# Last two expert pairs combined on chip by fp32r products, and the accumulating fetch issued one pair earlier

## The chip, the cores and the metric

The kernel runs on one core of one Trainium2 chip. The metric is the device time of one execution in microseconds (us), lower is better. Times come from repeated executions, and the stages are read from one execution that the hardware profiler recorded, with every instruction and every DMA packet.

## What is computed

Two layers of a diffusion transformer with 256 context and 512 latent tokens of width 1024. Each layer is a token mixer (recurrences and gated branches) followed by a mixture of 32 experts in which every token goes to two experts. The last layer keeps the 512 latent tokens alone. The part that matters here:

```python
def hier_moe(t, ...):                       # t: 768 tokens in layer 0, 512 in layer 1
    ...                                     # router: two experts and two weights per token
    def block_fn(args):
        e, tok = args
        xb = t_pad[tok]
        return (jax.nn.silu(xb @ w_gate[e]) * (xb @ w_up[e])) @ w_down[e]
    yb = lax.map(block_fn, (blk_e, slot_tok.reshape(n_blocks, MOE_BLOCK)))
    y = jnp.zeros((N + 1, D), F32).at[slot_tok].add(yb.reshape(-1, D).astype(F32) * slot_w[:, None])
    return y[:N]
...
xl = xl + mod_l[:, 5] * y                   # and, after layer 1, rmsnorm(xl, final_norm_g)
```

## The kernel before

Tokens lie in SBUF as `x2`, six tiles of 128 tokens by 1024 (four in layer 1). Each expert has 64 slots, and two experts make a pair, so there are 16 pairs (`NP`) of 128 slots. `moe` loops over the pairs. For a pair `j` the engines do this:

- SyncE (SP) streams the weights: for each pair six units of 2 MB (`unit`, L265: two for the first half of gate and up, two for the second, two for the down product) into a ring of tiles called `u` and `m`. The two down units of the last pair are split into pieces of 512 KB.
- TensorE (PE) computes gate and up into `gu` (L666), then the rows of pair `j + 1` are gathered by products with a 0/1 matrix `oh` (`gather`, tags `ext` and `ew`), then transposes of the hidden rows (`eht`, L677), then the down product `ey` (L685). `pair` runs in this order; the two `next(mid, None)` in it are where the work of the generator `mid` is put between gate/up and down.
- VectorE (DVE) scales the result by routing weight and modulation (`scale`, L843), and a POOL queue DMA stores it as 128 rows of `ys` in DRAM (L849, L854).

After the last pair but one, the outputs of pairs 0 to 14 lie in `ys`. `combine_most` then issues the *fetch*: for each of a token's two choices and each tile of tokens one indirect DMA on POOL's queue (L884) that reads 128 rows of `ys` and adds them to a tile of `x2`. That is 12 DMAs in layer 0 and 8 in layer 1, of 512 KB each. A choice that is not in `ys` reads the zero row `NYS`. The outputs of the last pair stay on chip: `oh` is transposed to `ohT`, and PE multiplies it with the scaled rows in plain fp32 (L866), six (four) tiles times two halves of 512 columns, and DVE adds each result to `x2` (L1301). These additions come after the fetch into the same tile.

Behind the experts of layer 0 comes the norm of layer 1 (`norm_next`) and its first projection. Behind those of layer 1 comes `combine`: squares on ScalarE (ACT), a few small DVE steps, a scaling of each tile and the store of the output (L1014). POOL multiplies two of the four tiles by the norm's gain ahead of time (L1005), so that ACT can scale those two while DVE scales the others.

A scheduler may interleave work that is independent; `pin` keeps an instruction in its place in the written order.

Of the kernel before, what the change touches and what calls it, by code (L numbers as in the profile page):

```python
# [21 lines left out]
D = 1024  # L22
# [15 lines left out]
NYS = NMAIN - 2 * CAP  # L38
# [20 lines left out]
class B:  # L59
# [121 lines left out]
    def layer(self, l):  # L181
# [5 lines left out]
        with pool(f"pp{l}", space=PSUM) as self.pp:  # L187
# [13 lines left out]
            with pool(f"hin{l}") as self.hp:  # L201
# [11 lines left out]
                cols = lambda t: t.rearrange("p a (b c) -> p (a b) c", c=256)  # L213
                M = []
                for g in self.groups:
                    if self.whole(g):
                        t = cols(self.buf(*g))
                        M.append((t[:, :KD], t[:, KD:]))
                    else:
                        M.append([cols(self.half(g, x)) for x in "ab"])  # L220
# [32 lines left out]
    def half(self, g, x):  # L253
        return g[0].tile([128, 2, 1024], F32R, name=g[1] + x)
# [31 lines left out]
    def merge(self, l, n, y, M):  # L286
        nc, d = self.nc, self.d
        hs = [(0, 384), (384, 384)] if n == T else [(0, 512)]
        with self.pool(f"mg{l}") as yp:
            y.append(self.y_in(7, n, yp))  # L290
            for dt in range(KD):
# [19 lines left out]
                for g, m in enumerate(M):  # L311
                    self.split(m[0][:, dt], m[1][:, dt], acc[:, 256 * g:256 * g + 256])
# [8 lines left out]
    def post(self, l, M):  # L321
# [4 lines left out]
        with self.pool(f"po{l}") as p:  # L326
# [33 lines left out]
            for lo in range(i0, NT, n):  # L360
# [12 lines left out]
                for dt in range(KD):  # L373
# [28 lines left out]
                    self.mm3(ps, [(wh[:, k, :], wl[:, k, :], M[g][0][:, k], M[g][1][:, k]) for k in range(KD)])  # L402
# [38 lines left out]
    def route(self, lo, n, p, pp, rows, lt, rb, ss, hook):  # L441
# [30 lines left out]
        if (lo - i0) % 4 == 0:  # L472
            g = self.groups[(lo - i0) // 4]
            self.low.append(self.buf(*g) if self.whole(g) else self.half(g, "a"))
# [97 lines left out]
        nc.vector.scalar_tensor_tensor(a, e2, E_ - 2.5, a, ALU.is_gt, ALU.max)  # L572
# [186 lines left out]

    def gather(self, j, oh, xr, xT, pp):  # L760
# [8 lines left out]
        self.nxt = xT, sw  # L769
        yield  # L770
# [26 lines left out]
    def moe(self, l, ew, mst):  # L797
        tc, nc, d, wp = self.tc, self.nc, self.d, self.wp
        cs = self.conds
        with self.pool(f"moep{l}", space=PSUM) as pp, self.pool(f"ewC{l}") as ewC:  # L800
# [29 lines left out]
            xr = self.thirds(rows.rearrange("p a b -> p (a b)") if l else self.r(self.half(self.groups[1], "b"))[:, 0])  # L830
            for j in range(NP):
                xT, sw = self.nxt
                if j + 1 < NP:
                    self.onehot(j + 1, oh, range(nt))
                    self.beside(j + 1, range(nt))
                    mid = self.gather(j + 1, oh, xr, xn, pp)
                else:
                    mid = self.combine_most(self.r(oh), pp)
                    next(mid)
                py = self.pair(xT, self.units[6 * j:6 * j + 6], wp, pp, mid, lambda i: load(n + 6 * j + 2 * i + 2))  # L840
                y = [part() for h in range(2)] if l else rows.rearrange("p (h a) b -> p h (a b)", h=2)
                yh = lambda h: y[h] if l else y[:, h]
                scale = lambda t, h, c: nc.vector.scalar_tensor_tensor(t, py[h], sw[:, c:c + 1], m5[c][h], ALU.mult, ALU.mult)  # L843
                if j + 1 < NP:
                    ys = self.ys[2 * CAP * j:2 * CAP * j + 2 * CAP]
                    for h in range(2):
                        scale(yh(h), h, 1)
                        if l:
                            nc.gpsimd.dma_start(ys[:, 512 * h:512 * h + 512], y[h])  # L849
                        else:  # L850
                            scale(tmp, h, 0)
# [23 lines left out]
    def combine_most(self, oh, pp):  # L875

        nc = self.nc
        nt, i0 = self.h2.shape[1], self.t_lo // 128

        slots = self.r(self.buf(*self.groups[0]))  # L880
        ohT, y0 = slots[:, 0].rearrange("p (i q) -> p i q", q=128), slots[:, 1].rearrange("p (h a) -> p h a", h=2)
        def fetch(s):
            for i in range(i0, NT):
                nc.gpsimd.indirect_dma_start(out=self.x2[:, i, :], out_offset=None, in_=self.ys[:],  # L884
                                             in_offset=bass.IndirectOffsetOnAxis(ap=self.idx[:, i, s:s + 1], axis=0),
                                             bounds_check=NYS, compute_op=ALU.add)

        fetch(0)
        yield
        for a in range(0, nt, 4):  # L890
            m = min(4, nt - a)
            ps = pp.tile([128, 4, 128], F32, name="ext", bufs=2)
            for i in range(m):
                nc.tensor.transpose(ps[:, i], oh[:, a + i], self.ident)
            nc.scalar.activation(ohT[:, a:a + m], ps[:, :m], AF.Copy)
        if not self.last:
            self.pre[0] = self.wload(self.wp, self.d["w_in"][self.l + 1, 0], 3, slots[:, 2].rearrange("p (a b) -> p a b", a=KD))
        fetch(1)
        yield
        yield  # L900
        yield ohT, y0
# [97 lines left out]
    def combine(self, p, gf):  # L999
        nc = self.nc  # L1000
        i0 = NCTX // 128
        ys = {}
        for i in (i0 + 1, i0 + 3):
            ys[i] = p.tile([128, D], F32, name=f"fny{i}")
            nc.gpsimd.tensor_tensor(ys[i], self.x2[:, i, :], gf, ALU.mult)  # L1005
        for a in range(i0, NT, 2):
            rs, xs = self.norms(p, range(a, a + 2), "fn", 4)
            for j, i in enumerate(range(a, a + 2)):
                f = rs[:, j:j + 1]
                if i in ys:  # L1010
                    nc.scalar.activation(xs[j], ys[i], AF.Copy, scale=f)
                else:
# [1056 lines left out]
```

## Time and profile before

| what | value |
|---|---|
| median of 3 runs | 2811.4 us (2807.12 to 2818.43) |
| profiled execution, its own time | 2813.25 us |
| span of its instructions | 2811.4 us |
| mean granted TensorE clock | 0.944 |
| busy: PE, DVE, ACT, POOL | 88%, 49%, 24%, 25% of the span |
| bytes moved by DMA | 667.05 MB |
| weights on queue q1; POOL's queue q0 | 54.5%; 6.3% of 16 engines' span |

The span is 1.85 us shorter than the profiled execution's own time: what lies around the instructions. The profile's page cuts the span into 40 slices of 70.3 us. The stage of the experts is slices 16 to 22 for layer 0 and 34 to 40 for layer 1. Busy shares are averages over stages with different limits, so the rows below are taken from the last two pairs of either layer and from what follows them.

### The profile page before, as it was taken

Reading aid. Unit: us, or ns where it says so; the run is one execution under the profiler, and the core shown is the slowest. Engines: PE = TensorE matmul, PEld = TensorE weight load, DVE = VectorE, ACT = ScalarE, POOL = GpSimd, SP = SyncE. Lnnn points to the kernel's source line nnn. Section 1 sums busy time; section 2 is a strip of 40 time slices with the busy share of each in tenths; the row PEclk is TensorE's granted clock in tenths of the full one; section 3 lists DMA queues with packets and bytes.
Section 4 is the critical chain, followed back from the end, with each engine's and each line's share of the span. In section 5 each row is a group of like instructions: output and inputs, shape, how many; then the busy total and the mean of one; then the engine's idle time right before and its main releaser. Section 6 shows DMA issues by size and latency. Waiting matters only on the chain. (4 is left out here: it accounts for less than half of the span.)

```text
span 2811.4 us, 39254 instructions
## 1 busy us (share of the span) xinstructions
PE 2477.0 (88%) x15674; PEld 1678.3 (60%) x15674; DVE 1374.0 (49%) x3210; ACT 664.9 (24%) x1322; POOL 695.8 (25%) x503
## 2 busy tenths in 40 slices
PE   4879999999999869999999599988999879999896
PEld 2657777777888644444444377777777654443342
DVE  8985467576566672122212436777564651111112
ACT  3332321222323431111111333222223421111111
POOL 3552332322323330000001424423224320000002
PEclk8989999999999879999999799899999889999998
DMA  5465443444257429999999533122228649999998
GB/s 210 171 207 179 157 155 122 126 141 138 90 194 248 139 86 379 419 422 422 421 420 411 152 98 125 50 70 83 74 92 286 214 190 420 422 422 422 420 421 272
DMA packets 176160, 667.05 MB, mean 237 GB/s; under 512 B 20672, under 2 KB 40800, under 8 KB 157920
## 3 DMA queue, kind: packets, MB, share of 16 engines
q1 hardware_dynamic: 152608, 586.19, 54.5%
q0 software_dynamic: 15072, 54.01, 6.3%
q10 hardware_dynamic: 8288, 24.27, 2.2%
q8 instruction: 124, 2.03, 0.3%
q14 instruction: 68, 0.56, 0.1%
HBM read 605.12 MB, written 61.38 MB: 237 GB/s over the span
## 5 line engine op out<-in xcount | busy, mean ns | idle before, releaser
L87 PE MATMUL mm<-hH,wh 128*128 128x512 f32 (+1 forms) x1408 | 521.9, 371 | 17.5 <-DVEq L905 6.4
L88 PE MATMUL mm<-hL,wh 128*128 128x512 f32 (+1 forms) x1408 | 510.4, 363 | 0.0
L85 PE MATMUL mm<-hH,wl 128*128 128x512 f32 (+1 forms) x1408 | 507.8, 361 | 2.7 <-POOL wl L79 2.7
L79 POOL TENSOR_TENSOR wl<-wraw,wh 128x1024 fp32r<-128x1024 f32 x117 | 317.2, 2713 | 769.3 <-ACT wh L78 683.3
L666 PE MATMUL gu<-u,wl 128*64 128x512 f32 x1664 | 466.4, 603 | 21.1 <-DMA u<-in_moe_wgu_dram 20.8
L87 PEld LDWEIGHTS mm<-hH,wh 128*128 128x128 f32 x1408 | 275.2, 195 | 85.4 <-issue 35.4
L85 PEld LDWEIGHTS mm<-hH,wl 128*128 128x128 f32 x1408 | 274.5, 195 | 47.2 <-issue 5.3
L666 PEld LDWEIGHTS gu<-u,wl 128*64 128x64 f32 x1664 | 153.0, 139 | 247.6 <-issue 214.2
L88 PEld LDWEIGHTS mm<-hL,wh 128*128 128x128 f32 x1408 | 275.5, 196 | 41.4 <-issue 5.4
L1301 DVE TENSOR_TENSOR wraw<-wraw,gu 128x512 f32<-128x512 f32 x64 | 44.0, 687 | 455.5 <-ACT wraw L671 452.2
L685 PE MATMUL ey<-u,wraw 128*64 128x512 f32 x960 | 230.0, 599 | 0.9 <-ACT wraw L679 0.9
L78 ACT ACTIVATE wh<-wraw 128x1024 fp32r<-128x1024 f32 x117 | 123.2, 1057 | 396.6 <-PE mm L88 296.8
L666 PE MATMUL gu<-m,wl 128*64 128x512 f32 x384 | 171.2, 599 | 22.7 <-DMA m<-in_moe_wgu_dram 22.7
L671 ACT ACTIVATE wraw<-gu 128x512 f32<-128x512 f32 x32 | 19.1, 597 | 657.9 <-PE gu L666 657.8
L685 PEld LDWEIGHTS ey<-u,wraw 128*64 128x64 f32 x960 | 71.2, 137 | 136.6 <-issue 134.1
L720 POOL CAST h<-W 128x8 fp32r<-128x8 f32 (+1 forms) x50 | 9.9, 197 | 554.6 <-PE ext L729 265.5
L728 PE MATMUL ext<-h,wh 128*128 128x384 f32 (+1 forms) x450 | 141.7, 327 | 0.0
L79 POOL TENSOR_TENSOR wl<-adaw,wh 128x512 fp32r<-128x512 f32 x58 | 96.4, 1679 | 168.5 <-ACT wh L78 154.6
L1059 PE MATMUL mm<-adaw,sc 128*32 128x256 f32 x768 | 86.8, 427 | 37.2 <-DMA adaw<-in_w_ada_dram 37.2
L666 PEld LDWEIGHTS gu<-m,wl 128*64 128x64 f32 x384 | 51.5, 138 | 108.8 <-issue 69.3
L729 PE MATMUL ext<-m,wh 128*128 128x384 f32 x360 | 110.3, 319 | 0.0
L728 PEld LDWEIGHTS ext<-h,wh 128*128 128x128 f32 x450 | 84.4, 188 | 24.3 <-issue 23.5
(642 smaller groups left out, 4127.7 us busy)
## 6 DMA issues: line engine op xcount, KB each, us to landing
u<-in_moe_wgu_dram SPq DMA_DIRECT2D x97, 2048.0 KB, 21.1
u<-in_moe_wd_dram SPq DMA_DIRECT2D x55, 2048.0 KB, 21.0
m<-in_moe_wgu_dram SPq DMA_DIRECT2D x24, 2048.0 KB, 23.9
adaw<-in_w_ada_dram SPq DMA_DIRECT2D x160, 256.0 KB, 3.5
wraw<-in_w_in_dram POOLq DMA_DIRECT2D x53, 512.0 KB, 4.0
wraw<-in_w_in_dram SPq DMA_DIRECT2D x27, 512.0 KB, 3.5
wraw<-in_w_out_dram SPq DMA_DIRECT2D x25, 512.0 KB, 3.5
adaw<-in_w_in_dram SPq DMA_DIRECT2D x50, 256.0 KB, 2.9
```

The source lines that it names most:

```text
L78: a = self.nc.scalar.activation(hi, src, AF.Copy)
L79: b = (eng or self.nc.vector).tensor_tensor(lo, src, self.r(hi), ALU.subtract)
L85: low = lambda i: nc.tensor.matmul(out, ops[i][1], ops[i][2], start=False, stop=i == len(ops) - 1)
L87: nc.tensor.matmul(out, lh, rh, start=i == 0, stop=False)
L88: nc.tensor.matmul(out, lh, rl, start=False, stop=False)
L666: self.pin(nc.tensor.matmul(ps[s], xT[:, k, s], w[2 * (k // 4) + u][:, k % 4, 512 * i:512 * i + 512], start=k == 0, stop=k == KD - 1))
L671: nc.scalar.activation(hh, gate, AF.Sigmoid)
L685: self.pin(nc.tensor.matmul(ps[s], hT[:, q, s], w[4 + u][:, q, 512 * h:512 * h + 512], start=q == 0, stop=q == 3))
L728: self.pin(self.nc.tensor.matmul(ps[:, :b - a], oh[:, i], self.h2[:, i, a:b], start=first and i == tiles[0], stop=False, skip_group_check= ...
L729: self.pin(self.nc.tensor.matmul(ps[:, :f - a], oh[:, i], self.lows(i)[:, a:f], start=False, stop=last and i == tiles[-1], skip_group_chec ...
L1059: nc.tensor.matmul(ps[32 * g:32 * g + 32, 256 * c:256 * c + 256], self.sc[:, k + q, 2 - 2 * m:34 - 2 * m], W[n][:, q, :], start=m == 0 and ...
L1301: self.nc.vector.tensor_tensor(o, a, b, op)
```

## The change

The rows in `ys` end two pairs earlier, at pair 13, and the zero row `NYS` moves with them. All indirect DMAs of the fetch are issued before pair 14 is computed, right behind the store of pair 13. The 0/1 matrices of pairs 14 and 15 are transposed as soon as their rows are gathered (`turn_onehot`). The scaled rows of pair 14, and later those of pair 15, are split into a high and a low fp32r part, and `combine_pair` multiplies both parts by the transposed matrix: for pair 14 inside pair 15 (between its gate/up and its down product), for pair 15 at the end. The tiles of one weight group are cut in three pieces instead of two to make room. In `combine`, POOL's early multiplication is dropped, and DVE scales all four tiles.

```diff
-NYS = NMAIN - 2 * CAP
+NYS = NMAIN - 4 * CAP
...
+    def turn_onehot(self, oh, ohT, pp):
+        nt = self.h2.shape[1]
+        for a in range(0, nt, 4):
+            m = min(4, nt - a)
+            ps = pp.tile([128, 4, 128], F32, name="ext", bufs=2)
+            for i in range(m):
+                self.pin(self.nc.tensor.transpose(ps[:, i], self.r(oh[:, a + i]), self.ident))
+            self.nc.scalar.activation(ohT[:, a:a + m], ps[:, :m], AF.Copy)
...
                 else:
-                    mid = self.combine_most(self.r(oh), pp)
-                    next(mid)
+                    mid = self.combine_pair(self.ohT[0], yp, pp, ("ext",))
+                if j == NP - 2:
+                    self.fetch()
                 py = self.pair(xT, self.units[6 * j:6 * j + 6], wp, pp, mid, lambda i: load(n + 6 * j + 2 * i + 2))
...
-                ohT, y0 = next(mid)
-                y = {1: [yh(h) for h in range(2)], 0: [y0[:, h] for h in range(2)]}
-                for c in cs:
-                    for h in range(2):
-                        scale(y[c][h], h, c)
-                for i in range(nt):
-                    it = i + self.t_lo // 128
-                    for h in range(2):
-                        ps = pp.tile([128, 512], F32, name="gu", bufs=2)
-                        nc.tensor.matmul(ps, ohT[:, i], y[int(it >= 2)][h], start=True, stop=True)
-                        x = self.x2[:, it, 512 * h:512 * h + 512]
-                        self.tt(x, x, ps, ALU.add)
+                y0, yp = self.buf(*self.groups[0]), {}
+                t = rows.rearrange("p (h a) b -> p h (a b)", h=2)
+                for i, c in enumerate(cs):
+                    yp[c] = y0[:, 2 * i], y0[:, 2 * i + 1]
+                    for h in range(2):
+                        w = slice(512 * h, 512 * h + 512)
+                        scale(t[:, h], h, c)
+                        self.split(yp[c][0][:, w], yp[c][1][:, w], t[:, h])
+            for _ in self.combine_pair(self.ohT[1], yp, pp, ("gu", "ext")):
+                pass
...
+    def combine_pair(self, ohT, yp, pp, tags):
+        n = 0
+        for i in range(self.h2.shape[1]):
+            it = i + self.t_lo // 128
+            y = yp[int(it >= 2)]
+            for h in range(2):
+                w = slice(512 * h, 512 * h + 512)
+                ps = pp.tile([128, 512], F32, name=tags[n % len(tags)], bufs=2)
+                n += 1
+                for a in range(2):
+                    self.pin(self.nc.tensor.matmul(ps, ohT[:, i], y[a][:, w], start=a == 0, stop=a == 1))
+                x = self.x2[:, it, w]
+                self.tt(x, x, ps, ALU.add)
+        yield
+        if tags == ("ext",) and not self.last:
+            raw = self.r(self.piece(self.groups[1], "b"))[:, 0].rearrange("p (a b) -> p a b", a=KD)
+            self.pre[0] = self.wload(self.wp, self.d["w_in"][self.l + 1, 0], 3, raw)
+        yield
...
-        for i in (i0 + 1, i0 + 3):
-            ys[i] = p.tile([128, D], F32, name=f"fny{i}")
-            nc.gpsimd.tensor_tensor(ys[i], self.x2[:, i, :], gf, ALU.mult)
...
-                if i in ys:
-                    nc.scalar.activation(xs[j], ys[i], AF.Copy, scale=f)
-                else:
-                    nc.vector.scalar_tensor_tensor(xs[j], self.x2[:, i, :], f, gf, ALU.mult, ALU.mult)
+                nc.vector.scalar_tensor_tensor(xs[j], self.x2[:, i, :], f, gf, ALU.mult, ALU.mult)
```

The first place is POOL's order at the end of layer 0's experts, before and then after; L720 and L721 (L717 and L718) write the routing weights beside the rows, `ys` is the store of a pair's output, and `x<-ys,idx` is the fetch.

```order
L721 TENSOR_TENSOR h_8861<-W,h_8861 128x4x2
L854 DMA ys<-wl 128x1024
L720 CAST h_8861<-W 128x2x2
L721 TENSOR_TENSOR h_8861<-W,h_8861 128x2x2
L720 CAST h_8861<-W 128x4x2
L721 TENSOR_TENSOR h_8861<-W,h_8861 128x4x2
L854 DMA ys<-wl 128x1024 x2
L884 DMA x_8851<-ys,idx 128x1024 x12
```

```order
L718 TENSOR_TENSOR h_8862<-W,h_8862 128x4x2
L871 DMA ys<-wl 128x1024
L717 CAST h_8862<-W 128x2x2
L718 TENSOR_TENSOR h_8862<-W,h_8862 128x2x2
L717 CAST h_8862<-W 128x4x2
L718 TENSOR_TENSOR h_8862<-W,h_8862 128x4x2
L871 DMA ys<-wl 128x1024
L894 DMA x_8852<-ys,idx 128x1024 x12
```

One of the two stores at the end (that of pair 14) is gone, and the twelve indirect DMAs follow the store of pair 13 directly.

The second place is PE's order in the last pair of layer 0, before and then after; `gu` is gate and up, `eht` the transposes of the hidden rows, `ey` the down product, and the last two rows combine.

```order
L666 MATMUL gu<-u_12662,wl 64x512
L666 MATMUL gu<-m_12664,wl 64x512
L677 MATMUL eht<-ident,wraw 128x128 x4
L685 MATMUL ey<-u_12755,wraw 64x512
L685 MATMUL ey<-u_12757,wraw 64x512
...
L866 MATMUL gu<-m_12772 128x512 x4
L866 MATMUL gu<-wl,m_12772 128x512 x8
```

```order
L663 MATMUL gu<-u_12710,wl 64x512
L663 MATMUL gu<-m_12712,wl 64x512
L909 MATMUL ext<-m_12824,m1c 128x512 x24
L674 MATMUL eht<-ident,wraw 128x128 x4
L682 MATMUL ey<-u_12814,wraw 64x512
L682 MATMUL ey<-u_12816,wraw 64x512
...
L909 MATMUL gu<-m_12954,m1a 128x512 x2
L909 MATMUL ext<-m_12954,m1a 128x512 x2
```

Twenty-four products for pair 14 now stand between gate/up and the transposes `eht`, in two PSUM buffers of the tag `ext`.

The third place is DVE's order over the same stretch of layer 0, before and then after; `wraw<-wraw,gu` are the two products that make the hidden rows, `ey` rows are the scalings, and `x` rows the additions to the tokens.

```order
L1301 TENSOR_TENSOR wraw<-wraw,gu 128x512 x2
L79 TENSOR_TENSOR wl<-m_12772,wh 128x1024
L843 SCALAR_TENSOR_TENSOR m_12772<-ey,sw,adaw 128x512
L843 SCALAR_TENSOR_TENSOR wl<-ey,sw,wh 128x512
...
L1301 TENSOR_TENSOR x_8851<-x_8851,gu 128x512 x6
L100 TENSOR_SCALAR n12v<-n12s 128x2
```

```order
L1309 TENSOR_TENSOR wraw<-wraw,gu 128x512
L1309 TENSOR_TENSOR x_8852<-x_8852,ext 128x512
L1309 TENSOR_TENSOR wraw<-wraw,gu 128x512
L1309 TENSOR_TENSOR x_8852<-x_8852,ext 128x512 x11
L79 TENSOR_TENSOR wl<-m1b,wh 128x1024
L858 SCALAR_TENSOR_TENSOR wl<-ey,sw,adaw 128x512 x2
L79 TENSOR_TENSOR m_12954<-wl,m_12954 128x512
L858 SCALAR_TENSOR_TENSOR wl<-ey,sw,wh 128x512
L79 TENSOR_TENSOR m_12954<-wl,m_12954 128x512
L1309 TENSOR_TENSOR x_8852<-x_8852,gu 128x512
```

One addition of pair 14 stands between the two products of the hidden rows and eleven behind them, and the splits into two parts (L79) are new.

## Rows read from the trace of the kernel before

**Rows 1.** The page's part 2, 40 slices of the span.

```profile
DMA  5465443444257429999999533122228649999998
GB/s 210 171 207 179 157 155 122 126 141 138 90 194 248 139 86 379 419 422 422 421 420 411 152 98 125 50 70 83 74 92 286 214 190 420 422 422 422 420 421 272
```

**Rows 2.** Waits of PE over the experts of layer 0: total, times, longest.

```profile
PE gu L666 <- DMA m<-in_moe_wgu_dram: 17.2, 14, 3.0
```

**Rows 3.** Four windows: engines' busy time, granted clock, DMA share, GB/s.

```profile
1512.00:1530.00 18.00, 18.00 (x102) 10.29 (x102) 5.05 (x11) 3.88 (x9) 0.15 (x1) 1.00 1.00 421
1545.00:1559.00 14.00, 9.16 (x33) 3.18 (x30) 3.86 (x5) 1.06 (x1) 9.40 (x7) 0.92 1.06 219
2742.00:2756.00 14.00, 13.63 (x77) 6.94 (x77) 2.12 (x6) 3.36 (x8) 1.08 (x2) 1.00 1.01 427
2770.00:2780.00 10.00, 8.90 (x34) 3.19 (x35) 0.57 (x1) 0.66 (x2) 4.42 (x3) 0.83 1.06 252
```

**Rows 4.** DMA queues from 1550 to 1590 us: packets, MB, share of 16 engines.

```profile
q0 software_dynamic: 1359, 4.92, 61.9%
q1 hardware_dynamic: 1324, 4.26, 28.0%
```

**Rows 5.** Timeline of POOL, end of layer 0's experts: start, duration, count, idle.

```profile
1496.80 0.57 POOL L854 DMA_DIRECT2D ys<-wl  x1 [11.95 <-DVE wl L1301]
1529.85 0.54 POOL L854 DMA_DIRECT2D ys<-wl  x1 [32.48 <-DVE wl L1301]
1538.01 1.71 POOL L884 DMA_INDIRECT x<-ys,idx  x1 [7.62 <-issue]
1563.23 1.57 POOL L884 DMA_INDIRECT x<-ys,idx  x1 [1.32 <-DMA x<-ys,idx]
```

**Rows 6.** Timeline of PE, last pair of layer 0, and the next layer's first product.

```profile
1534.46 0.64 PE L666 MATMUL gu<-m,wl 128*64 128x512 f32 x1 [0.56 <-DMA m<-in_moe_wgu_dram]
1542.93 0.66 PE L677 MATMUL eht<-ident,wraw 128*128 128x128 f32 x4 [1.39 <-DVE wraw L1301]
1544.06 7.87 PE L685 MATMUL ey<-u,wraw 128*64 128x512 f32 x32 [0.47 <-ACT wraw L679]
1609.05 0.55 PE L87 MATMUL mm<-hH,wh 128*128 128x256 f32 x1 [6.43 <-DVEq L905]
```

**Rows 7.** Timeline of DVE, last pair of layer 0 and the additions.

```profile
1541.39 1.48 DVE L1301 TENSOR_TENSOR wraw<-wraw,gu 128x512 f32<-128x512 f32 x2 [11.85 <-ACT wraw L671]
1566.69 1.28 DVE L1301 TENSOR_TENSOR x<-x,gu 128x512 f32<-128x512 f32 x2 [8.00 <-DMA x<-ys,idx]
1585.69 0.68 DVE L1301 TENSOR_TENSOR x<-x,gu 128x512 f32<-128x512 f32 x1
```

**Rows 8.** Timeline of POOL, end of layer 1's experts.

```profile
2764.00 1.72 POOL L884 DMA_INDIRECT x<-ys,idx  x1 [8.93 <-issue]
2784.67 1.57 POOL L884 DMA_INDIRECT x<-ys,idx  x1 [0.71 <-DMA x<-ys,idx]
```

**Rows 9.** Timeline of PE, last pair of layer 1.

```profile
2762.15 0.64 PE L666 MATMUL gu<-m,wl 128*64 128x512 f32 x1 [0.99 <-DMA m<-in_moe_wgu_dram]
2771.75 9.50 PE L685 MATMUL ey<-u,wraw 128*64 128x512 f32 x32 [0.47 <-ACT wraw L679]
```

**Rows 10.** Timeline of DVE, end of layer 1: additions and the final scalings.

```profile
2786.99 1.29 DVE L1301 TENSOR_TENSOR x<-x,gu 128x512 f32<-128x512 f32 x2 [4.95 <-DMA x<-ys,idx]
2795.72 0.68 DVE L1301 TENSOR_TENSOR x<-x,gu 128x512 f32<-128x512 f32 x1
2800.05 1.28 DVE L1013 SCALAR_TENSOR_TENSOR fnx<-x,fnr,gf 128x1024 f32<-128x1024 f32 x1
2803.41 1.28 DVE L1013 SCALAR_TENSOR_TENSOR fnx<-x,fnr,gf 128x1024 f32<-128x1024 f32 x1
```

**Rows 11.** Groups of DVE by shape over the whole span: count, busy us, mean ns.

```profile
L843 DVE SCALAR_TENSOR_TENSOR adaw<-ey,sw,wh 128x512 f32<-128x512 f32 x32 | 24.0, 751 | 119.7 <-PE ey L685 117.6
L79 DVE TENSOR_TENSOR wl<-adaw,wh 128x512 fp32r<-128x512 f32 x30 | 21.0, 718 | 19.7 <-PE mm L85 19.7
L1301 DVE TENSOR_TENSOR x<-x,gu 128x512 f32<-128x512 f32 x20 | 13.4, 684 | 26.7 <-DMA x<-ys,idx 23.0 <-PE gu L866 3.6
```

More of the change, by code (lines that the diff above doesn't have):

```diff
@@ L211, in layer @@
                 self.units = []
-                cols = lambda t: t.rearrange("p a (b c) -> p (a b) c", c=256)
                 M = []
                 for g in self.groups:
-                    if self.whole(g):
-                        t = cols(self.buf(*g))
-                        M.append((t[:, :KD], t[:, KD:]))
-                    else:
-                        M.append([cols(self.half(g, x)) for x in "ab"])
+                    ts = [self.buf(*g)] if self.whole(g) else [self.piece(g, x) for x in "abc"]
+                    t = [t[:, a, 256 * b:256 * b + 256] for t in ts for a in range(t.shape[1]) for b in range(4)]
+                    M.append((t[:KD], t[KD:]))
                 self.merge(l, n, y, M)
@@ L251, in whole, with piece @@
         return self.last or g[1] != "m1"
-    def half(self, g, x):
-        return g[0].tile([128, 2, 1024], F32R, name=g[1] + x)
+    def piece(self, g, x):
+        return g[0].tile([128, 1 + (x == "a"), 1024], F32R, name=g[1] + x)
     def unit(self, n):
@@ L311, in merge @@
                 for g, m in enumerate(M):
-                    self.split(m[0][:, dt], m[1][:, dt], acc[:, 256 * g:256 * g + 256])
+                    self.split(m[0][dt], m[1][dt], acc[:, 256 * g:256 * g + 256])
     def bcast(self, dst, row):
@@ L401, in post @@
                     ps = pp.tile([128, 512], F32, name="mm", bufs=3)[:, :N]
-                    self.mm3(ps, [(wh[:, k, :], wl[:, k, :], M[g][0][:, k], M[g][1][:, k]) for k in range(KD)])
+                    self.mm3(ps, [(wh[:, k, :], wl[:, k, :], M[g][0][k], M[g][1][k]) for k in range(KD)])
                     px = pp.tile([128, 512], F32, name="S", bufs=2)
@@ L473, in route @@
             g = self.groups[(lo - i0) // 4]
-            self.low.append(self.buf(*g) if self.whole(g) else self.half(g, "a"))
+            self.low.append(self.buf(*g) if self.whole(g) else self.piece(g, "a"))
         def h2(i):
@@ L769, in gather @@
         self.nxt = xT, sw
+        if j >= NP - 2:
+            if self.last:
+                ohT = self.wp.tile([128, 4, 128], F32R, name="adaw", bufs=3)
+            else:
+                ohT = self.piece(self.groups[1], "ca"[j + 2 - NP]).rearrange("p a (i q) -> p (a i) q", q=128)
+            self.turn_onehot(oh, ohT, pp)
+            self.ohT.append(ohT)
         yield
@@ L828, in moe @@
             xn = self.r(wp.tile([128, KD, 128], F32R, name="wl", bufs=2))
-            xr = self.thirds(rows.rearrange("p a b -> p (a b)") if l else self.r(self.half(self.groups[1], "b"))[:, 0])
+            xr = self.thirds(rows.rearrange("p a b -> p (a b)") if l else self.r(self.piece(self.groups[1], "b"))[:, 0])
+            self.ohT = []
+            yp = None
             for j in range(NP):
@@ L873, in moe @@
         self.over = l, nb, self.t_lo, cs
[L875 to L888, printed above, removed]
-        yield
[L890 to L898, printed above, removed]
@@ new lines, in fetch @@
+    def fetch(self):
+        for s in range(2):
+            for i in range(self.t_lo // 128, NT):
+                self.nc.gpsimd.indirect_dma_start(out=self.x2[:, i, :], out_offset=None, in_=self.ys[:],
+                                                  in_offset=bass.IndirectOffsetOnAxis(ap=self.idx[:, i, s:s + 1], axis=0),
+                                                  bounds_check=NYS, compute_op=ALU.add)
+    def combine_pair(self, ohT, yp, pp, tags):
[11 more added lines that the diff above has]
+                self.tt(x, x, ps, ALU.add)
+        yield
+        if tags == ("ext",) and not self.last:
+            raw = self.r(self.piece(self.groups[1], "b"))[:, 0].rearrange("p (a b) -> p a b", a=KD)
+            self.pre[0] = self.wload(self.wp, self.d["w_in"][self.l + 1, 0], 3, raw)
@@ L899, in combine_most @@
         yield
-        yield
-        yield ohT, y0
     def overflow(self, w, again):
```

12 lines of the change are left out of this document (5 added, 7 removed).

## The prediction

> **What bounds the kernel now.** I looked first at the slices of the page. Over the experts of either layer the DMA engines are full and the weights come at 419 to 422 GB/s [rows 1]. PE is nearly full there too, so the next question was who waits for whom: in 14 of layer 0's 16 pairs PE stops for a weight unit, 17.2 us in all [rows 2]. The stream of weights sets the pace, and PE has a little to spare.
>
> Then I read the ends of the two stages. Take the moment at which the last gate/up unit of the last pair lands and its products begin; I call it M. In layer 0 M is 1534.46, the down product begins 9.6 us later and ends at 1551.93 [rows 6]. In layer 1 M is 2762.15 and the down product runs from 2771.75 to 2781.25 [rows 9]. What follows is not PE: the first addition to the tokens waits 8.00 us for the fetch in layer 0 and starts at 1566.69 [rows 7], and 4.95 us in layer 1 [rows 10]. The fetch is issued from 1538.01 to 1563.23 and from 2764.00 to 2784.67 [rows 5, 8], after M in both layers. So before, nearly all of the fetch is transferred behind the weights, and the last addition ends at 1586.37 and 2796.40 [rows 7, 10].
>
> **What the fetch costs the DMA engines.** This decides the case. With weights alone the DMA share is 1.00 to 1.01 and the rate 421 to 427 GB/s; with the fetch it is again full, at 1.06, but the rate falls to 219 and 252 GB/s [rows 3]. The queues of 1550 to 1590 us agree: q0 needs 61.9% of 40 us for 4.92 MB, 5.0 us per MB, against 2.6 us per MB on q1 [rows 4]. The shares add up to 1.06 where both are full, so I divide: 4.75 us per MB. One indirect DMA of 512 KB (0.524 MB) thus takes all sixteen engines for 2.5 us. The fetch is 29.9 us of full DMA time in layer 0 (12) and 19.9 us in layer 1 (8).
>
> Moving it one pair ahead puts it into a stretch where the engines are already full. In layer 0 the store of pair 13 is issued at 1496.80, and before, the fetch followed its store by 8.2 us (1529.85 to 1538.01) [rows 5]; so it will be issued from about 1505, some 29 us ahead of M. Every microsecond that it takes is taken from weights which M still needs. The ring of weight tiles can't absorb that: it was drained at every pair, as PE's waits say. Given back is the store of pair 14, 0.524 MB at 421 GB/s, 1.2 us. M moves by 29.9 - 1.2 = 28.7 us to 1563.2 in layer 0, and by 18.7 us to 2780.9 in layer 1.
>
> The Trainium skill has a rule on this ("DMA: Bandwidth & Descriptors", Issuing engines are not separate DMA queues): transfers started by different engines run on the same 16 DMA engines, and another issuing engine saves only issue time. By it POOL's queue is no extra road, which is what the fall from 421 to 219 GB/s at a full share shows [rows 3], and the sum below stands; were it wrong here, the sum would be that of the first rival.
>
> **From M to the last addition, after the change.** The hidden rows' first product starts 6.93 us after M as before (1541.39) [rows 6, 7]. DVE then has product, addition, product, and the remaining additions of pair 14. PE has the combining products of pair 14 ahead of the transposes `eht` and only two PSUM buffers for them, so `eht` waits until all but two additions are done. Additions run at 0.64 us each (1.28 for two) [rows 7]; the fp32r products under them are no longer than these, for one such pair is two passes where an addition reads 512 columns (estimate, no row has this shape). Layer 0: 6.93 + 2.0 for the first three steps + 9 x 0.64 + 0.55 for the last product = 15.3. From `eht` to `ey` it is 1.13 us [rows 6], so `ey` starts 16.4 us after M (9.6 before). Layer 1, with eight additions: 6.93 + 2.0 + 5 x 0.64 + 0.55 + 1.13 = 13.9. The down product takes 7.1 us (7.87 and 9.50 before, where the fetch delayed its weights [rows 6, 9]), which gives M + 23.5 and M + 21.0.
>
> The first scaling starts 0.8 us before that end, as one half is ready early. DVE then has, in layer 0, 4 scalings of 0.75, 4 splits of 0.72 and 12 additions of 0.64 [rows 7, 11]: 13.5 us. In layer 1 it is 2, 2 and 8: 8.1 us. The fetch is long done. The last addition ends at 1563.2 + 23.5 - 0.8 + 13.5 = 1599.4 in layer 0 (13.0 later than before) and at 2780.9 + 21.0 - 0.8 + 8.1 = 2809.2 in layer 1 (12.8 later).
>
> **The rest.** From the last addition to layer 1's first projection there were 22.7 us [rows 6, 7]. The same DVE steps follow now in another order; I take no difference, with 1 us either way. In `combine` the scalings leave POOL and ACT: before, the last addition was 8.3 us ahead of the end of the last scaling (2796.40 to 2804.69) [rows 10]. Now DVE has four scalings of 1.28 instead of two beside two on ACT, two more in its own line, against a step that POOL's multiplication stretched; I take +1.3 us, between 0 and 2.6. The transposes of the 0/1 matrices (6 and 4 per pair) and the splits of pair 14 fall into time in which PE and DVE wait for weights; without that cover the splits would be 4 x 0.72 + 2 x 0.72 = 4.3 us [rows 11]. The layer's next weights (`w_in`) now have ACT's first step ahead of the `eht` copies; they are the last on the weights' queue, some 11 us after M, and the copies are due at 15, so this costs nothing unless they land 4 us late.
>
> **Sum.** 13.0 + 12.8 + 1.3 = 27.1 us. The profiled execution took 2813.25 us, its span 2811.4, and the median is 2811.4; the sum on the profiled one is 2840.4, on the median 2838.5. I say 2839.
>
> **Rivals.** *The fetch is hidden under the weights after all* (if its time were waiting and not engine time). Then M comes 1.2 us early and the rest is as above: layer 0's last addition at 1569.5 (16.9 earlier), layer 1's at 2789.3 (7.1 earlier), less 1.3: 22.7 us faster, 2789. For it: q1 goes on moving bytes while q0 runs [rows 4]. Against it: the rate falls to half at a full share [rows 3]. It decides the sign if less than 46% of the fetch's time is charged to the weights (22.7 of the 49.8 us between the two cases).
>
> *Half charged*: part of the fetch's time is waiting that weights can use. By the same line (-22.7 + 49.8 times the share charged), 30 to 70% charged gives 8 us faster to 12 us slower, 2803 to 2823. For it: the shares add up to 1.06, so a little overlap there is [rows 3]; against it: no more than that.
>
> *The weights keep the right of way and the fetch trickles.* Then M stays, but the additions of pair 14, in front of `eht`, wait for the fetch. The down units are 4 MB behind M, 10 us at 421 GB/s, and the fetch would end 29.9 and 19.9 us later, near 1574 and 2792. With `ey` about 2 us behind that, 7.1 us of it and the tail, the last additions end near 1596 and 2807: 9.6 + 10.6 + 1.3 = 21 us slower, 2832. Against it: when the fetch ran, the rate of all queues together fell from 427 to 252 GB/s while the last weights were still under way (the down product of layer 1 runs in that window) [rows 3, 9].
>
> *A colder TensorE*: PE stands still while the fetch runs and fills little of the combining stretch. In layer 1 before, the clock was 0.83 from 2770 to 2780 and `ey` took 9.50 us instead of 7.1 [rows 3, 9]. Two such products would add 4.8 us: 2844.
>
> **Numbers.** 14 us is 0.5%, about what a measurement of this kernel tells from no change. Full charge, warm or cold TensorE: 0.70, slower. Weights first: 0.08, slower. Half charged: 0.12, same by its middle. Hidden: 0.10, faster. So faster 0.10, same 0.12, slower 0.78. The likeliest case alone is 2830 to 2850: 2.3 to 2.75 us per indirect DMA is -4 to +5 us, the cold clock +5, the tails 2 each way. The range of 8 in 10 reaches down over part of the half-charged case: 2814 to 2852.
>
> **What would show it.** Right: layer 0's indirect DMAs start near 1505, the weights' GB/s fall to about half for 30 us there; M is near 1563 in layer 0 and, with that layer's 13 us, near 2794 in layer 1; `eht` waits 5 to 6 us for additions; no addition waits for the fetch. Wrong: M less than 15 us later in layer 0 (the engines had room), or additions of pair 14 that wait for the fetch, or a last addition less than 36 us after M, which would say that the tail is shorter than I built it.

## The result and the profile after

The changed kernel takes 2829.5 us (median of 4 runs, 2828.4 to 2832.0) where the kernel before takes 2809.3 beside it (median of 4, 2805.9 to 2818.4): a ratio of 1.0075, with a 95% interval of 1.0053 to 1.0097. It is slower by 20 us; 2839 was predicted, 2814 to 2852 the range.

Between the two ends that the change moves, from layer 1's first projection to its last pairs of experts, the profiled executions of the kernels below that keep the fetch spread over 1104 to 1117 us, in no order that follows their edits. So I read the traces from the issue of the store of pair 13, called S below (layer 0: 1496.80 before [rows 5], 1500.03 after; layer 1: 2720.71 and 2726.30). From S to layer 1's first projection it is 112.3 us before and 122.5 after; from layer 1's S to the end of the span 90.7 and 101.7. Together that is 21.2 us more, about the difference of the medians. Every stretch in this document comes from one execution.

POOL's timeline of the changed kernel, layer 0 (start, duration, what it is, idle time before it and what ended that), which answers to [rows 5]:

```profile
1500.03 0.57 POOL L871 DMA_DIRECT2D ys<-wl  x1 [13.24 <-DVE wl L1309]
1508.29 1.71 POOL L894 DMA_INDIRECT x<-ys,idx  x1 [7.69 <-DMA ys<-wl]
...
1521.22 1.57 POOL L894 DMA_INDIRECT x<-ys,idx  x1 [1.82 <-DMA x<-ys,idx]
1528.63 1.57 POOL L894 DMA_INDIRECT x<-ys,idx  x1 [5.83 <-DMA x<-ys,idx]
...
1552.50 1.57 POOL L894 DMA_INDIRECT x<-ys,idx  x1 [2.24 <-DMA x<-ys,idx]
```

The fetch starts 8.3 us after S, as predicted, but it takes 44 us to issue: a second choice adds to the tile that a first choice has added to, and waits up to 5.9 us for it. The DMA queues of 1512 to 1548 us (packets, MB, share of the 16 engines' time) show who had the engines in that time, to be read beside [rows 4]:

```profile
DMA packets 1642, 12.28 MB, mean 341 GB/s; under 512 B 159, under 2 KB 159, under 8 KB 1137
q1 hardware_dynamic: 859, 9.38, 63.0%
q0 software_dynamic: 782, 2.88, 40.1%
```

The engines are full, and the fetch costs 40.1% of 36 us for 2.88 MB, 5.0 us per MB as before the change. But it gets only 40% of them; the weights keep 63%. Counted in packets the two queues are nearly even, 782 and 859.

PE's timeline in layer 0, which answers to [rows 6]:

```profile
1551.58 1.11 PE L663 MATMUL gu<-m,wl 128*64 128x512 f32 x1 [6.01 <-DMA m<-in_moe_wgu_dram]
...
1568.37 1.33 PE L909 MATMUL ext<-m,m1c 128*128 128x512 f32 x4 [0.39 <-DVE x L1309]
1572.54 2.08 PE L909 MATMUL ext<-m,m1c 128*128 128x512 f32 x4 [2.84 <-DVE x L1309]
1574.41 1.06 PE L674 MATMUL eht<-ident,wraw 128*128 128x128 f32 x4
1579.32 9.73 PE L682 MATMUL ey<-u,wraw 128*64 128x512 f32 x32 [3.85 <-ACT wraw L676]
```

M is 1551.58, S + 51.6 (37.7 before). The products of pair 14 then wait for additions that wait for the fetch, and the down product waits for ACT. DVE's timeline (which answers to [rows 7]) and ACT's say why:

```profile
1567.63 1.29 DVE L1309 TENSOR_TENSOR x<-x,ext 128x512 f32<-128x512 f32 x2 [0.44 <-DMA x<-ys,idx]
1571.80 1.29 DVE L1309 TENSOR_TENSOR x<-x,ext 128x512 f32<-128x512 f32 x2 [2.89 <-DMA x<-ys,idx]
1575.27 1.28 DVE L1309 TENSOR_TENSOR x<-x,ext 128x512 f32<-128x512 f32 x2 [2.18 <-DMA x<-ys,idx]
...
1600.20 0.68 DVE L1309 TENSOR_TENSOR x<-x,ext 128x512 f32<-128x512 f32 x1
```

```profile
1577.94 1.06 ACT L78 ACTIVATE wh<-m1b 128x1024 fp32r<-128x1024 f32 x1 [16.59 <-DMA m1b<-in_w_in_dram]
1578.90 0.64 ACT L676 ACTIVATE wraw<-eht 128x256 f32<-128x256 f32 x2
```

`w_in`, last on the weights' queue, lands at S + 77.9, and ACT's step on it stands ahead of the `eht` copies. In layer 1 no addition waits for the fetch, but M comes late there too; PE's rows, which answer to [rows 9]:

```profile
2780.57 1.11 PE L663 MATMUL gu<-m,wl 128*64 128x512 f32 x1 [6.09 <-DMA m<-in_moe_wgu_dram]
...
2796.63 0.60 PE L674 MATMUL eht<-ident,wraw 128*128 128x128 f32 x4
```

### The profile page after: what moved, and what is told of

It is laid out like the page before. It is cut to its first block, busy times and chain, and to the rows that moved or that the text cites. A ratio compares the mean times of both kernels' runs of the same rounds, so it can differ in the third digit from the quotient of the medians.

```text
span 2828.0 us, 39400 instructions
## 1 busy us (share of the span) xinstructions
PE 2484.2 (88%) x15724; PEld 1681.6 (59%) x15724; DVE 1389.6 (49%) x3242; ACT 670.4 (24%) x1335; POOL 683.7 (24%) x498
## 5 line engine op out<-in xcount | busy, mean ns | idle before, releaser
L87 PE MATMUL mm<-hH,wh 128*128 128x512 f32 (+1 forms) x1408 | 519.9, 369 | 17.1 <-ACT sg L1653 6.2
L79 POOL TENSOR_TENSOR wl<-wraw,wh 128x1024 fp32r<-128x1024 f32 x117 | 316.0, 2703 | 770.7 <-ACT wh L78 683.8
L663 PE MATMUL gu<-u,wl 128*64 128x512 f32 x1664 | 476.7, 612 | 28.4 <-DMA u<-in_moe_wgu_dram 27.1
L663 PE MATMUL gu<-m,wl 128*64 128x512 f32 x384 | 178.6, 620 | 34.1 <-DMA m<-in_moe_wgu_dram 34.1
L668 ACT ACTIVATE wraw<-gu 128x512 f32<-128x512 f32 x32 | 19.1, 597 | 668.3 <-PE gu L663 625.7
L717 POOL CAST h<-W 128x8 fp32r<-128x8 f32 (+1 forms) x50 | 9.6, 192 | 555.3 <-PE ext L726 267.0
L79 POOL TENSOR_TENSOR wl<-adaw,wh 128x512 fp32r<-128x512 f32 x58 | 93.8, 1634 | 162.8 <-ACT wh L78 150.1
L725 PEld LDWEIGHTS ext<-h,wh 128*128 128x128 f32 x450 | 84.4, 188 | 24.3 <-issue 22.7
## 6 DMA issues: line engine op xcount, KB each, us to landing
u<-in_moe_wgu_dram SPq DMA_DIRECT2D x97, 2048.0 KB, 22.7
```

The lines of the kernel that those rows point to most:

```text
L79: b = (eng or self.nc.vector).tensor_tensor(lo, src, self.r(hi), ALU.subtract)
L87: nc.tensor.matmul(out, lh, rh, start=i == 0, stop=False)
L663: self.pin(nc.tensor.matmul(ps[s], xT[:, k, s], w[2 * (k // 4) + u][:, k % 4, 512 * i:512 * i + 512], start=k == 0, stop=k == KD - 1))
L668: nc.scalar.activation(hh, gate, AF.Sigmoid)
L725: self.pin(self.nc.tensor.matmul(ps[:, :b - a], oh[:, i], self.h2[:, i, a:b], start=first and i == tiles[0], stop=False, skip_group_check= ...
```

## Experiments

The theories. **Theory 1**: the fetch stands in front of the weights, and costs in full what it takes of the DMA engines. **Theory 2**: the new order behind M (24 products and 12 additions of pair 14 ahead of `eht`) is the cost. **Theory 3**: ACT's step on `w_in` ahead of the `eht` copies. **Theory 4**: the final norm's scalings. All times from S, in us:

| kernel | ratio to before (95%) | M, layer 0 / 1 | last addition ends, 0 / 1 | layer 1's first projection | end of span |
|---|---|---|---|---|---|
| before | 1 | 37.7 / 41.4 | 89.6 / 75.7 | 112.3 | 90.7 |
| changed | 1.0075 (1.0053 to 1.0097) | 51.6 / 54.3 | 100.9 / 85.6 | 122.5 | 101.7 |
| before_nofetch | stretches only | 37.5 / 39.7 | 67.1 / 66.8 | 89.5 | - |
| after_nofetch | stretches only | 36.3 / 37.9 | 72.6 / 66.4 | 94.4 | - |
| after_plain | 1.0000 (0.9978 to 1.0022) | 44.6 / 46.5 | 83.9 / 76.8 | 105.9 | 92.9 |
| merged | 1.0066 (1.0041 to 1.0092) | 51.6 / 54.0 | 94.1 / 84.5 | 115.0 | 102.5 |
| win_late | 1.0083 (1.0057 to 1.0108) | 50.8 / 54.6 | 94.4 / 85.4 | 116.2 | 101.5 |
| old_combine | 1.0088 (1.0059 to 1.0116) | 51.6 / 54.0 | 101.1 / 85.5 | 122.8 | 101.4 |
| fetch_behind | 1.0025 (1.0011 to 1.0039) | 35.4 / 38.4 | 89.0 / 75.1 | 110.8 | 91.1 |
| late_fetch | 0.9959 (0.9944 to 0.9975) | 36.9 / 36.4 | 87.0 / 68.0 | 108.0 | 83.9 |
| plain_late | 0.9970 (0.9952 to 0.9989) | 35.6 / 38.0 | 82.4 / 72.2 | 102.7 | 87.0 |
| hybrid | 0.9961 (0.9947 to 0.9975) | 36.1 / 38.2 | 84.5 / 71.5 | 106.5 | 86.4 |
| mixed | 0.9930 (0.9914 to 0.9945) | 37.5 / 37.9 | 78.6 / 66.5 | 99.8 | 81.3 |

A total and its two stretches needn't agree to the microsecond: over this table the totals lie between 1 us below and 9 us above what the two stretches add up to, both taken against the kernel before (win_late 9, fetch_behind 8).

**The fetch left out** of the changed kernel, and of the kernel before (there its two calls of `fetch`).

```
-                if j == NP - 2:
-                    self.fetch()
```

> The changed kernel with the accumulating fetch left out (the tokens lack what the first 14 pairs give). Theory 1, the fetch in front of the weights is the whole cost: M comes back by 13 to 15 us in layer 0 (M about 36.5 us behind the store of pair 13) and by 12 to 13 us in layer 1; without the waits of additions for the fetch too, about 44 us faster than the changed kernel (near 2785). Theory 2, the new order behind M (24 products and 12 additions of pair 14 ahead of eht, then splits and 12 more additions) has a price of its own: this kernel is then 8 to 15 us slower than the kernel before with its fetch left out; by theory 1 alone the two are within 3 us of each other.

> The kernel before with the accumulating fetch left out (the tokens lack what the first 15 pairs give). Its additions no longer wait: layer 0's last addition 20 to 25 us earlier (about 1562), layer 1's about 12 us earlier, so some 35 us faster than the kernel before (near 2774). If the fetch costs the same wherever it stands, the changed kernel without its fetch gains the same 35 us over the changed one; by theory 1 (dearer in front of the weights) it gains at least 15 us more than this.

Without the fetch layer 1 gets other tokens, sends them to other experts and runs blocks of its overflow, so the totals (2937.5 and 2934.8) say nothing; the stretches do. S, `w_in` and the last addition of layer 0 in the changed kernel without the fetch, then S and the last addition in the kernel before without it:

```profile
1493.95 0.57 POOL L869 DMA_DIRECT2D ys<-wl  x1 [13.24 <-DVE wl L1307]
...
1541.62 1.06 ACT L78 ACTIVATE wh<-m1b 128x1024 fp32r<-128x1024 f32 x1 [4.51 <-DMA m1b<-in_w_in_dram]
...
1565.91 0.68 DVE L1307 TENSOR_TENSOR x<-x,ext 128x512 f32<-128x512 f32 x1
```

```profile
1497.44 0.57 POOL L854 DMA_DIRECT2D ys<-wl  x1 [11.95 <-DVE wl L1299]
...
1563.90 0.69 DVE L1299 TENSOR_TENSOR x<-x,gu 128x512 f32<-128x512 f32 x1
```

The fetch costs 28.2 us in layer 0 of the changed kernel (100.85 less 72.63) and 19.1 in layer 1 (85.55 less 66.42); in the kernel before it costs 22.4 (89.57 less 67.15) and 8.8. So it is dearer in front of the weights by 5.8 and 10.3 us. The order behind M by itself, with no fetch in either, costs 5.5 us in layer 0 and nothing in layer 1 (0.4 less). That lies between what I had set for theory 1 alone (within 3) and for theory 2 (8 to 15): both keep a share in layer 0; layer 1 is theory 1 alone. M comes back by 15.3 and 16.4 us, more than expected in layer 1 (12 to 13). For the kernel before I had expected some 35 us; it is 31.3.

**A fetch that overwrites** (`compute_op=ALU.add` taken out of the call).

> The changed kernel with a fetch that overwrites the tokens instead of adding to them (the result lacks the residual). Theory 1, engine time, and half of it is the accumulation: q0's time per MB falls from 5.0 us to near 2.6, M comes 6 to 7 us earlier in each layer, no addition waits for the fetch in layer 0, 15 to 20 us faster than the changed kernel (near 2812). Rival, the fetch is slow by its order and its waits and not by the addition in the DMA: q0's time per MB stays at 5, and the time within 5 us of the changed kernel.

The queues of 1512 to 1548 us of this kernel:

```profile
DMA packets 2384, 15.08 MB, mean 419 GB/s; under 512 B 239, under 2 KB 239, under 8 KB 1872
q1 hardware_dynamic: 1248, 10.89, 72.4%
q0 software_dynamic: 1135, 4.17, 28.8%
```

28.8% of 36 us for 4.17 MB is 2.5 us per MB, half of the accumulating fetch, and all queues together are back at 419 GB/s. M comes 7.0 and 7.7 us earlier, and the time is 17 us below the changed kernel's (2812.2), both about as expected. That is engine time, charged to the weights; the rival falls.

**Both pairs combined at the end**, the outputs of pair 15 in a slot of the ring; `win` holds only the step on `w_in`, behind the `eht` copies.

```
-                    mid = self.combine_pair(self.ohT[0], yp, pp, ("ext",))
+                    mid = self.win()
...
+                ms = [(o[:, i], yp[int(it >= 2)][a]) for o, yp in zip(self.ohT, yps) for a in range(2)]
+                for k, (o, y) in enumerate(ms):
+                    self.pin(self.nc.tensor.matmul(ps, o, y[:, w], start=k == 0, stop=k == len(ms) - 1))
```

> The changed kernel, the fetch where the change has it, but the products of both last pairs in one stretch behind the down product, four fp32r products into one PSUM tile and one addition each (12 additions in layer 0 instead of 24). Theory 1 alone: M stays 13 to 14 us late, and the additions never were the cost, so the time stays within 4 us of the changed kernel. Theory 2, the order behind M is the cost: eht follows M at 9 to 10 us, from M to the last addition 30 to 35 us instead of 48.7 in layer 0 and 25 to 27 instead of 31.3 in layer 1, 15 to 24 us faster than the changed kernel (2806 to 2815), though M stays late.

M to `eht` falls to 11.4 us (22.8 in the changed kernel), and yet only 6.7 us of layer 0's and 1.1 of layer 1's last addition come back, and the total hardly moves: theory 2 falls short. PE's rows show the next wait:

```profile
1562.06 0.66 PE L674 MATMUL eht<-ident,wraw 128*128 128x128 f32 x4 [1.40 <-DVE wraw L1313]
1563.19 5.35 PE L682 MATMUL ey<-u,wraw 128*64 128x512 f32 x16 [0.47 <-ACT wraw L676]
1569.84 1.04 PE L682 MATMUL ey<-u,wraw 128*64 128x512 f32 x2 [1.30 <-DMA u<-in_moe_wd_dram]
1573.30 5.34 PE L682 MATMUL ey<-u,wraw 128*64 128x512 f32 x14 [2.41 <-DMA u<-in_moe_wd_dram]
```

The down product starts early and waits for its own weights, the last of which let it go on at S + 74.2. What M did not lose to the fetch, the down units lost: the product ends at S + 79.5, against 55.1 before.

**`w_in` behind the `eht` copies**, by pinning both in program order on ACT.

> The changed kernel with the first step of the next layer's projection weights (w_in, on ACT) behind the eht copies instead of ahead of them; nothing else moves. Theory 3, the eht copies wait for these weights: the down product of the last pair of layer 0 starts 3 to 4 us earlier (eht to ey 1.1 us instead of 4.9), and the stretch from the store of pair 13 to layer 1's first projection falls from 122.5 to about 119 us; 3 to 4 us of the total, less than its noise. Rival, the down product would have waited for its own weights anyhow: ey starts earlier but ends within 1 us of where it did.

The down product starts 3.8 us earlier and, with TensorE at full speed, ends 6.5 us earlier (S + 82.6 for 89.0); layer 0's stretch falls by 6.4 us, where 3 to 4 were expected. The rival falls; but the total does not show the gain (1.0083).

**The final norm's scalings as before.**

> The changed kernel with the final norm's scalings as before (two on POOL and ACT, two on DVE). Theory 4, that part of the change is a term of its own: from the last addition to the end of the span 15.0 us instead of 16.1, about 1 us of the total, under its noise. Rival: no difference in that stretch.

From the last addition to the end it is 15.9 us, where the changed kernel has 16.1 and the kernel before 15.0. The scalings are not that microsecond. DVE's rows of the kernel before and then of the changed one show what else differs; `fnv` is the first of the norm's small steps, and the last addition of the kernel before ends at 2796.40 [rows 10]:

```profile
2794.40 0.30 DVE L100 TENSOR_SCALAR fnv<-fns 128x2 f32<-128x2 f32 x1
...
2796.50 2.34 DVE L108 SCALAR_TENSOR_TENSOR fny<-fnt,fni 128x2 f32<-128x2 f32 x1
```

```profile
2811.18 0.68 DVE L1309 TENSOR_TENSOR x<-x,ext 128x512 f32<-128x512 f32 x1
2811.77 0.16 DVE L100 TENSOR_SCALAR fnv<-fns 128x2 f32<-128x2 f32 x1
```

Before, the small steps begin 2.0 us ahead of the last addition's end, in the gaps between additions that still wait; in the changed kernel they begin right at that end. Over the table, the end takes 14.8 to 15.1 us where they begin 1.9 to 2.8 us ahead (before, plain_late, hybrid, mixed), and 15.9 to 18.0 where they don't. The microsecond goes with that start; no run moves the start alone. The two scalings that DVE took over are about made up for by the step of 2.34 us beside POOL's multiplication, which the changed kernel no longer has.

**Only the fetch's wait moved.** The fetch is emitted behind the additions of pair 14; on every engine the instructions stand in the changed kernel's order.

```
-                if j == NP - 2:
-                    self.fetch()
...
+        if tags == ("ext",):
+            self.fetch()
         yield
```

> The changed kernel with one thing undone: the fetch waits until DVE has added the products of the last pair but one (each engine's instructions stand in the same order as in the changed kernel; only what POOL waits for differs). Theory 1: M back to 36 to 38 us behind the store of pair 13 in layer 0 and 37 to 40 in layer 1, no addition of pair 14 waits for the fetch, the fetch runs behind the weights, and the last addition comes 80 to 89 us behind that store in layer 0 (100.8 in the changed kernel, 89.6 before) and 68 to 75 in layer 1 (85.6 and 75.7): 2792 to 2808, near or under the kernel before. Theory 2 (the combining stretch of pair 14 ahead of eht is a cost of the same size, whatever the fetch does): the stretch from M to eht stays 16 us, and the time stays over 2815.

POOL's first issue, PE's `eht` and `ey`, ACT's step on `w_in`, and DVE's first addition behind the fetch and its last:

```profile
1538.05 1.71 POOL L892 DMA_INDIRECT x<-ys,idx  x1 [44.79 <-DVE x L1309]
```

```profile
1544.51 0.60 PE L674 MATMUL eht<-ident,wraw 128*128 128x128 f32 x4
1545.58 7.09 PE L682 MATMUL ey<-u,wraw 128*64 128x512 f32 x32 [0.47 <-ACT wraw L676]
```

```profile
1539.56 1.06 ACT L78 ACTIVATE wh<-m1b 128x1024 fp32r<-128x1024 f32 x1 [4.53 <-DMA m1b<-in_w_in_dram]
```

```profile
1563.09 0.69 DVE L1309 TENSOR_TENSOR x<-x,gu 128x512 f32<-128x512 f32 x1 [7.62 <-DMA x<-ys,idx]
...
1580.97 0.68 DVE L1309 TENSOR_TENSOR x<-x,ext 128x512 f32<-128x512 f32 x1
```

This decides between the theories, by the stretches. M is back at 35.4 and 38.4; `eht` still follows 16.4 us behind M in layer 0, and the loss is gone in both stretches (110.8 and 91.1, for 112.3 and 90.7 before). The order behind M costs nothing when the fetch runs beside it. `w_in` lands at S + 46.9 instead of S + 77.9. The total, 2813.0 (1.0025), misses the expected 2792 to 2808: it takes back 14 of the 21 us, and is 7 us above before, which these stretches (together 1.1 us below it) don't hold. The two profiled executions don't hold it either (2809.6 us, and 2813.3 for the kernel before), so where it lies stays open.

**Combined at the end and held back.** As merged, with the fetch behind a tiny POOL copy that reads the last gate/up unit.

```
+                    g = nc.gpsimd.tensor_copy(gt, self.r(self.units[6 * j + 3][0:1, 3, 0:1]))
+                    with tc.issue_after(g.ins):
+                        self.fetch()
```

> As merged, and the fetch held back on POOL until the last gate/up unit of the last pair has landed. Theory 1 (the fetch ahead of the weights, and the chain that hangs on the weights, are the cost): M back to 36 to 38 us behind the store of pair 13 in layer 0 and 38 to 40 in layer 1, the down product of layer 0 ends near M + 18, and the last addition comes 86 to 91 us behind that store in layer 0 (89.6 before, 94.1 merged) and 73 to 77 in layer 1 (75.7 before, 84.5 merged): within 5 us of the kernel before, 2803 to 2811, some 15 us faster than merged. Rival, the splits, the fp32r products in two parts and the one long combining stretch cost by themselves: M is early and the time stays over 2816.

Only the fetch's start differs from merged, and the time is 28 us under merged's (2796.4 for 2824.5), 0.4% faster than before; 15 us and 2803 to 2811 were expected, and layer 1's last addition comes at 68.0 instead of 73 to 77. Against the kernel before, where the fetch stands behind the store of pair 14, it starts 3.2 and 5.8 us earlier after S.

**Without the addition in the DMA**, three ways: rows into free slots of the ring and added by DVE.

```
+                b = self.r(self.buf(*self.ring[(6 * NP - 6 + k // 4) % n]))
+            t = b[:, k % 4]
+            self.nc.gpsimd.indirect_dma_start(out=t, out_offset=None, in_=self.ys[:],
...
+        for x, t in rows:
+            self.pin(self.nc.vector.tensor_tensor(x, x, t, ALU.add))
```

> As merged, with the fetch issued once the first half of the last pair's gate/up products is done, and without the addition in the DMA: the rows go into the slots of the ring that are free by then (12 or 8 tiles), and DVE adds them while it waits for the down product. If theory 1 is right in both its parts (engine time at 2.5 us per MB instead of 5.0, and the shortest chain behind what is transferred last), the last addition comes 72 to 80 us behind the store of pair 13 in layer 0 (89.6 before) and 66 to 71 in layer 1 (75.7 before): 12 to 22 us faster than the kernel before, 2786 to 2797. Rival, DVE's 12 and 8 more additions or the shared port of DVE and POOL eat it: within 5 us of the kernel before.

> Layer 0 as plain_late, with the second six of DVE's additions behind the scalings and splits of the last pair; layer 1 as late_fetch. Expected 75 to 81 us from the store of pair 13 to the last addition in layer 0 (82.4 in plain_late) and 67 to 69 in layer 1: 2784 to 2793, 12 to 20 us faster than the kernel before. Rival: DVE is the bound in any order, the stretch of layer 0 stays at 82 and the time at 2791 to 2796.

> As plain_late, but only the first choices go plainly into free slots and are added by DVE; the second choices are added in the DMA behind that. DVE's excess over the kernel held back (12 additions of 1.2 us) is halved, the DMA engines' time is 3/4 of that of late_fetch. If both bounds seen in plain_late (DVE) and late_fetch (DMA) are real, the last addition comes 76 to 82 us behind the store of pair 13 in layer 0 (87.0 in late_fetch, 82.4 in plain_late) and 65 to 69 in layer 1 (68.0 and 72.2): 2784 to 2794. Rival: the second choices wait for DVE's additions and bring back waits of 2 to 3 us per tile: no better than late_fetch, 2796.

plain_late gains where the DMA was the bound (layer 0, 4.6 us better than late_fetch) and loses in layer 1 (4.1 us worse), where the down product ends 3.2 us later (M is 1.6 us later, and it waits for its last weights) and the last of DVE's eight additions of 1.2 us stand ahead of the scalings: a miss by its bounds on both stretches, though the time (2796.7) lies inside. hybrid missed too (2796.2): layer 0's last addition is 2.1 us later than in plain_late; the six additions put behind the scalings (6.9 us) now stand in front of the last twelve. Its layer 1, arranged as in late_fetch, takes 71.5 where that took 68.0: differences of that size between these kernels need not be their order. mixed splits the work, lies within all its bounds (2787.4 us) and is the best kernel here, 0.7% faster than before. Its second choices still wait for DVE, on POOL:

```profile
1544.35 1.00 POOL L899 DMA_INDIRECT u<-ys,idx  x1 [0.30 <-issue]
1547.09 1.60 POOL L899 DMA_INDIRECT x<-ys,idx  x1 [1.74 <-DVE x L925]
1549.33 1.58 POOL L899 DMA_INDIRECT x<-ys,idx  x1 [0.64 <-DVE x L925]
```

## Why the prediction was right, and where it was off

**The charge in full: right.** 29.9 and 19.9 us of engine time were to be taken from the weights. In layer 0 `w_in`, the last load on the weights' queue, lands 30.2 us later than without the fetch (77.9 against 47.7) and 31.0 us later than with the fetch behind (46.9). The rivals "hidden" and "half charged" fall. The rule of the Trainium skill that stood beside this ("DMA: Bandwidth & Descriptors", Issuing engines are not separate DMA queues) holds here: POOL's transfers took 40% of the time of the same 16 engines.

**M: the term that was mis-sized.** "Every microsecond that it takes is taken from weights which M still needs" is the step that failed. M moved by 13.9 and 12.8 us from before, not 28.7 and 18.7 (15.3 and 16.4 from the same kernel without the fetch). The two queues share the engines, and the fetch's own waits stretch it, so when M's weights had landed a part of it was still to come. POOL's queue from the fetch's first issue to M, in layer 0 (1508.29 to 1551.58) and in layer 1 (2736.27 to 2780.56):

```profile
q0 software_dynamic: 912, 3.35, 38.7%
```

```profile
q0 software_dynamic: 927, 3.40, 38.5%
```

That is 3.35 of 6.29 MB and 3.40 of 4.19, or 16.8 and 17.1 us of the engines, about what M lost. What was left fell on the down units and `w_in`. The sharing could have been read before the change: with both queues busy they moved 1359 and 1324 packets [rows 4]. Two of the prediction's own three signs of being wrong came true, M less than 15 us later in layer 0 and additions of pair 14 that wait for the fetch.

**From M to the last addition: right without the fetch.** Built were 36.2 and 28.3 us; without the fetch they are 36.4 and 28.5. Layer 0's is a little luck: the products let two additions through every 1.5 us, not every 1.28, so the scalings start 1.1 us later than built, and what follows them is 0.9 us shorter. In the changed kernel they are 49.3 and 31.3. Layer 0's 12.9 us more are 6.4 ahead of `eht` (2.8 in slow gate/up products, the rest in additions that wait for the fetch, which I had excluded), 3.8 for `w_in` (which I had priced at nothing unless 4 us late) and 2.6 in a slow down product; layer 1's 2.8 are slow gate/up products. So the rival of the trickling fetch had the right waits beside a late M, and the colder TensorE was there as well, with 8.3 us in place of 4.8. (That rival's layer 1 adds up to 2808.4, not 2807, and its time to 2834. And the 9.50 us of `ey` were not all clock: layer 0's `ey` took 7.87 at a granted clock of 1.00.)

**The number: partly luck.** M was forecast 14.8 and 5.9 us too late, and the way from M to the last addition 13.1 and 3.0 too short, so the errors nearly cancel. In sum the last additions come 28.2 and 19.1 us later than without the fetch, near the 29.9 and 19.9 of engine time; but 5.5 and 2.8 us of that are products at the lower clock, which the sum did not hold, and in layer 1 the last 0.8 MB of the fetch cost nothing.

**The order behind M** I counted as a cost beside the fetch. It is one only where nothing else lasts as long: 5.5 us without a fetch, none with the fetch behind it.

**The rest.** From the last addition to layer 1's first projection 21.7 us for 22.7; at the end 1.1 us for the 1.3 predicted, but not by the scalings: it goes with the later start of the norm's small steps, which the prediction did not have. In sum 10.3 + 10.9 = 21.2 us for 27.1.

**Where the gain was.** The accumulating fetch takes about the same engine time wherever it stands (46.5% of 67.7 us from 1508.29 to 1576 in the changed kernel, 31.5 us; 76.6% of 43.0 us from 1538.05 to 1581 in fetch_behind, 32.9). What differs is the chain behind the last transfer: behind the fetch the two additions of one tile (fetch_behind: last fetch packet at S + 87.2, last addition at 89.0), behind the weights the whole of the down product, scalings, splits and additions (changed: fetch done at S + 74.8 and `w_in` at 77.9, last addition at 100.9). In fetch_behind the last of these transfers ends 9 us later, and the last addition 12 us earlier.

## What to carry to other kernels

Where the DMA engines are full, as here, moving a transfer ahead only decides which one comes last: put last the one with the shortest chain behind it. Charge an early transfer to everything that shares the engines until it is done, not only to the next thing waited for, and expect the two queues to share rather than to take turns. An accumulating fetch cost twice the engine time of a plain one here (5.0 against 2.5 us per MB); where an engine stands idle behind it, take plain rows for a part and add them there (mixed, 0.7% faster than before).

## What the runs showed of the hardware

An indirect DMA that accumulates took 5.0 us of all engines' time per MB, one without 2.5; on POOL an issue took 1.57 us against 1.01. With both queues busy in front of M, q0 had 40.1% of the engines and q1 63.0%; behind M in the kernel before it was 61.9 and 28.0% [rows 4], at nearly even packet counts in both places.

Waits of 6 us cost PE more than their length. Behind the 6.0 us wait at M single products took 1.06 us at first and 0.59 later, at a granted clock of 0.50 (1551.58 to 1556.5) and 1.00 (1557.6 to 1561.5), the lower and the upper of the clock's two levels (1.2 and 2.4 GHz). The same 31 gate/up products took 9.94 us at a granted clock of 0.71 behind a 6.0 us wait, and 7.10 at 1.00 without it (in layer 1, behind 6.1 us, 9.93 at 0.72 against 7.10); first the changed kernel's windows, then those of after_nofetch (stretch, us, busy of PE, PEld, DVE, ACT, POOL, clock, DMA share, GB/s):

```profile
1551.58:1561.52 9.94, 9.94 (x31) 2.90 (x31) 0.13 (x1) 0.60 (x1) 1.57 (x1) 0.71 1.06 275
```

```profile
1530.20:1537.30 7.10, 7.10 (x31) 2.29 (x31) 0.15 (x1) 0.60 (x1) 0.00 (x0) 1.00 1.02 404
```
